# Sliding-window attention in a two-layer decoder kernel: value differences in place of two selects, weight splits on VectorE, and constants placed in earlier memory

## The chip, the cores and the metric

The kernel runs on one core of one Trainium2 chip, in one launch. The metric is the device time in microseconds; the median over several runs counts. Beside these runs one execution is profiled, and all rows below are from that execution.

## The reference

Two layers work on 512 rows of 1024 columns in fp32: an mLSTM layer, then a sliding-window attention layer with 16 query heads on 4 key/value heads, each layer with a post-norm, a squared-ReLU MLP (4096 wide) and a gated embedding. The change touches the attention layer. Cut to it:

```python
def swa_sink_attention(x, pos, k_sh, v_sh, w_q, b_q, sinks, w_o, b_o):
    q = partial_rope((x @ w_q + b_q).reshape(B, S, 16, 64), pos)
    kb, vb = banded(k_sh, nb), banded(v_sh, nb)      # block before, own block: 2 x 128 rows
    scores = einsum('bnqkgd,bnskd->bnkgqs', q, kb) * 64 ** -0.5
    diff = qi + 128 - si                             # qi: 0..127, si: 0..255
    valid = (diff >= 0) & (diff < 128) & (not before the first row)
    scores = where(valid, scores, -inf)
    m = maximum(max(scores), sink)
    e = exp(scores - m)
    probs = e / (sum(e) + exp(sink - m))
    out = einsum('bnkgqs,bnskd->bnqkgd', probs, vb).reshape(B, S, 1024)
    return out @ w_o + b_o
```

A query at place q of its block of 128 rows sees, of the block before, the places s > q, and of its own block, the places s <= q. So for each place s exactly one of the two blocks is seen.

## The kernel before

Rows come in four tiles of 128 (t = 0 to 3). Every product that needs fp32 is made of three matmuls (`mm3`, lines 88 to 90): the high and the low part of the weight against the high and the low part of the data, without low by low. So each weight matrix of 128 x 1024 is loaded into `wraw` (SyncE's DMA queue, line 83), and `split` makes `whi` from it on ScalarE (line 76) and `wlo` as the difference on another engine (line 77). `load_w` takes that engine as an argument: VectorE by default, GpSimd for `w_kv`, `w_q` and the first half of `w_o`. There are three `wraw` buffers and six each of `whi` and `wlo`.

The order of instructions on each engine is not the order of the code: a scheduler in the build sets it, engine by engine, and each engine then works through its own row in order. Memory is handed out by pools that open and close like a stack from the left or the right side; a tile in a pool opened later waits, tile by tile, for the last use of what lay in the same place.

The stage ahead of the attention layer is the first layer's gated embedding (`ple`, lines 709 to 737). Its tiles `pj` and `xr` lie in the pool `ps7`, along with the MLP's operands `S1`, `S23`, `S4A` and `T`, which are no longer used by then. When that pool closes, `pk` opens in its place, for what the attention layer keeps: the keys `KH` and `KL`, the values `vph` and `vpl` (high and low, one of each per tile), the biases `kvb` and `bq`. Value tiles have 64 zero columns ahead of and behind each head's 64, so that one matmul can write one head into the upper and another into the lower half of the output; these zeros are written by GpSimd (line 755).

The key/value projection then runs over four tiles (lines 792 to 811) into two accumulator banks. VectorE adds the bias out of the bank (`kv`, line 796) and rotates the keys (lines 779 to 782); TensorE transposes them (line 803), and ScalarE and VectorE write them as `KH` and `KL`.

Then, for each of the four key/value heads, `q_group` computes the queries (line 824 adds their bias, GpSimd rotates them, lines 833 and 834 write them into `QS`), and `attend` does the attention of a head's four query heads on one tile. In `attend` the scores of both blocks are computed, and VectorE copies the block before into the own block where the mask says so (line 850). So a row holds 128 scores, each of one block or the other. VectorE takes the maximum (line 851), and lines 856 to 859 make from it the maximum with the sink, its negative, and the exponent of the sink. ScalarE takes the exponentials (line 865), TensorE transposes the probabilities (line 873), and `ah` and `al` are their high and low parts. The two blocks' parts are taken apart again by four selects on GpSimd (lines 884 and 887), and each goes with its block's values (lines 893 to 895). The attend of one head and the query groups of the next are mixed by the scheduler.

Of the kernel before, what the change touches and what calls it, by code (L numbers as in the profile page):

```python
# [10 lines left out]
F32 = mybir.dt.float32  # L11
F32R = mybir.dt.float32r
# [3 lines left out]
ALU = mybir.AluOpType  # L16
# [14 lines left out]
KVH = 4  # L31
HD = 64
# [7 lines left out]
ASCALE = 0.125  # L40
# [5 lines left out]
def yoco_kernel(ctx: ExitStack, tc: tile.TileContext, A: dict, out: bass.AP):  # L46
    nc = tc.nc
    V, ACT, PE, GP = nc.vector, nc.scalar, nc.tensor, nc.gpsimd

    def pool(name, bufs=1, stack=ctx, **kw):  # L50
        return stack.enter_context(tc.tile_pool(name=name, bufs=bufs, **kw))

    base = pool("base")
# [14 lines left out]
    def tp_bank():  # L68
        return bank("tp")

    def f32(t):
        return t.bitcast(F32)


    def split(raw, n, hi, lo, eng=V):
        ACT.copy(hi, raw)  # L76
        eng.tensor_sub(lo, raw, f32(hi))  # L77

    def load_w(src, n, eng=V):
        raw = wpool.tile([P, 1024], F32, tag="raw", name="wraw", bufs=3)  # L80
        hi = wpool.tile([P, 1024], F32R, tag="whi", name="whi", bufs=6)
        lo = wpool.tile([P, 1024], F32R, tag="wlo", name="wlo", bufs=6)
        nc.sync.dma_start(raw[:, :n], src)
        split(raw[:, :n], n, hi[:, :n], lo[:, :n], eng)
        return hi, lo

    def mm3(o, lh, ll, rh, rl, start, stop):
        PE.matmul(o, lh, rh, start=start, stop=False)  # L88
        PE.matmul(o, lh, rl, start=False, stop=False)  # L89
        PE.matmul(o, ll, rh, start=False, stop=stop)  # L90
# [323 lines left out]
    sinkb = base.tile([P, KVH, 2, 2], F32, name="sinkb")  # L414
# [72 lines left out]
    sp = {}  # L487
# [44 lines left out]

    def seven_pools(i, side):
        sctx7 = ExitStack()
        ps = sp["s"] = pool(f"ps7{i}", stack=sctx7, side=side, reuse_waits="tile")
        sp["S1"] = [ps.tile([P, 4, 256], F32R, name=f"S1{x}") for x in "hl"]
        sp["S23"] = [ps.tile([P, 2, 4, 256], F32R, name=f"S23{x}") for x in "hl"]
        sp["S4A"] = [ps.tile([P, 2, 4, 256], F32R, name=f"S4A{x}") for x in "hl"]
        sp["T"] = ps.tile([P, 2, 512], F32, name="T")
        return sctx7  # L540
# [205 lines left out]
    pk = pool("pk", stack=kctx, side="right", reuse_waits="tile")  # L746
    KH = pk.tile([P, KVH, S], F32R, name="KH")
    KL = pk.tile([P, KVH, S], F32R, name="KL")
    VW = HD * (2 * KVH + 1)
    vph = [pk.tile([P, VW], F32R, name=f"vph{t}") for t in range(NT)]  # L750
    vpl = [pk.tile([P, VW], F32R, name=f"vpl{t}") for t in range(NT)]
    for t in range(NT):
        for vv in (vph[t], vpl[t]):
            for j in range(KVH + 1):
                GP.memset(f32(vv)[:, 2 * HD * j:2 * HD * j + HD], 0.0)
    kvb = pk.tile([P, 512], F32, name="kvb")
    nc.gpsimd.dma_start(kvb, A["kv_b"].partition_broadcast(P))
# [14 lines left out]
    pb = pool("pb", stack=bctx, side="right", reuse_waits="tile")  # L772
# [16 lines left out]
            mm3(ps, XH[:, k, tsl(t)], XL[:, k, tsl(t)], wh[:, sl], wl[:, sl], k == 0, k == KD - 1)  # L789
        return ps  # L790

    w = [load_w(A["w_kv"][0, c], 1024, GP) for c in range(4)]
    for t in range(NT):
        ps = proj512(t, w)
        kv = pb.tile([P, 512], F32, tag="bh", name="kv", bufs=2)
        V.tensor_add(kv, ps, kvb)  # L796
        kk = kv[:, 0:256].rearrange("p (h d) -> p h d", d=HD)
        rope(kk, t, KVH, V)
        kd = pb.tile([P, KVH, 2, HD], F32, tag="bl", name="kd", bufs=2)
        ACT.copy(kd, kk.unsqueeze(2).broadcast_to([P, KVH, 2, HD]))  # L800
        pt = tp_bank()
        for h in range(KVH):
            PE.transpose(pt[:, tsl(h)], kd[:, h].rearrange("p a d -> p (a d)"), ident)
        pv = pt.rearrange("p (h s) -> p h s", s=P)
        ACT.copy(KH[:, :, tsl(t)], pv)
        V.tensor_sub(KL[:, :, tsl(t)], pv, f32(KH)[:, :, tsl(t)])
        v = kv[:, 256:512].rearrange("p (h d) -> p h d", d=HD)
        vh = vph[t][:, HD:].rearrange("p (h d) -> p h d", d=2 * HD)[:, :, 0:HD]
        vl = vpl[t][:, HD:].rearrange("p (h d) -> p h d", d=2 * HD)[:, :, 0:HD]
        ACT.copy(vh, v)  # L810
        V.tensor_sub(vl, v, vh.bitcast(F32))
# [24 lines left out]
    def attend(gi, t):  # L836
        scs = []
        smax = pb.tile([P, 2, 2], F32, tag="smax", name="smax", bufs=2)
        for pr in range(2):
            k0 = max(t - 1, 0) * P  # L840
            ps = bank("sc")
# [9 lines left out]
            V.tensor_reduce(smax[:, :, pr], cur, AX.X, ALU.max)  # L851
            scs.append(cur)
        sk = sinkb[:, gi].rearrange("p pr par -> p par pr")
        m = pb.tile([P, 2, 2], F32, tag="am", name="am", bufs=2)
        nm = pb.tile([P, 2, 2], F32, tag="anm", name="anm", bufs=2)
        V.scalar_tensor_tensor(m, smax, ASCALE, sk, ALU.mult, ALU.max)
        V.tensor_scalar(nm, m, -1.0, None, ALU.mult)
        es = pb.tile([P, 2, 2], F32, tag="es", name="es", bufs=2)
        V.tensor_sub(es, sk, m)
# [14 lines left out]
        ah = pb.tile([P, 4, P], F32R, tag="ah", name="ah", bufs=2)  # L874
        al = pb.tile([P, 4, P], F32R, tag="al", name="al", bufs=2)
        pTv = pT.rearrange("p (h q) -> p h q", q=P)
        ACT.copy(ah, pTv)
        V.tensor_sub(al, pTv, f32(ah))
        parts = []
        if t > 0:  # L880
            bh = pb.tile([P, 4, P], F32R, tag="bh", name="bh", bufs=2)
            bl = pb.tile([P, 4, P], F32R, tag="bl", name="bl", bufs=2)
            for o, i_ in ((bh, ah), (bl, al)):
                GP.affine_select(out=o, in_=f32(i_), pattern=[[0, 4], [-1, P]], compare_op=ALU.is_ge, fill=0.0, base=-1, channel_multiplier=1)
            parts.append((t - 1, bh, bl))
            for o in (ah, al):
                GP.affine_select(out=o, in_=f32(o), pattern=[[0, 4], [1, P]], compare_op=ALU.is_ge, fill=0.0, base=0, channel_multiplier=-1)
        parts.append((t, ah, al))
        po = bank("pt")
        for i_, (kb, h_, l_) in enumerate(parts):  # L890
            for par in range(2):
                c0 = 2 * HD * gi + (HD if par == 0 else 0)
                mm3(po[:, :256], vph[kb][:, c0:c0 + P], vpl[kb][:, c0:c0 + P],
                    h_[:, 2 * par:2 * par + 2, :], l_[:, 2 * par:2 * par + 2, :],
                    i_ == 0 and par == 0, i_ == len(parts) - 1 and par == 1)
        pov = po[:, :256].rearrange("p (a q) -> p a q", a=2)
# [2 lines left out]
        V.tensor_sub(dl, pov, f32(dh))  # L899

    def load_q(gi):
        return [load_w(A["w_q"][gi, c], 1024, GP) for c in range(2)]

    w = load_q(0)
    for t in range(NT):
        q_group(0, t, w)
    for gi in range(KVH - 1):
        w = load_q(gi + 1)
# [121 lines left out]
```

## Time and profile before

| | us |
|---|---|
| three runs | 1225.95, 1220.97, 1225.16; median 1225.16 |
| profiled execution, its own time | 1223.72 |
| its span, first to last instruction | 1222.0 |
| TensorE busy | 1185.8 (97%) |
| VectorE busy | 877.2 (72%) |
| ScalarE busy | 586.6 (48%) |
| GpSimd busy | 148.1 (12%) |
| mean granted clock of TensorE | 0.991 of full speed |

In the rows, PE is TensorE, PEld its weight loads, DVE VectorE, ACT ScalarE, POOL GpSimd and SP SyncE. A row of the timeline gives the start and the duration in us, the engine, the line, the operation, what is written and read, a count where equal neighbours are merged, and in brackets the idle time ahead of it and what ended that. A row of the windows view gives for a stretch of time its length, then busy time and count of each engine, the granted clock, the DMA share and GB/s. Matmuls overlap, so the step from one start to the next says what one costs. The attention layer lies between about 600 and 800 us.

### The profile page before, as it was taken

The page shows a single profiled execution, that of the slowest core. Times are in us where ns is not written, and L with a number is a line of the kernel's source. Part 1 is how long each engine was busy: PE and PEld are TensorE (multiplying, and loading weights), DVE is VectorE, ACT ScalarE, POOL GpSimd, SP SyncE. Part 2 cuts the span into 40 slices and gives each one's busy share as a digit, 9 for nine tenths or more (in the row PEclk, how much of TensorE's full clock was granted, in tenths as well). Part 3 has the DMA queues.
Part 4 walks back from the last instruction along what each step waited for, and adds up shares of the span by engine and source line. Part 5 has one row for each costly group of instructions (what it writes and reads, how often), then busy time and mean ns, then how long its engine had stood idle before and what let it go on. Part 6 is the DMA issues. An engine that isn't in the chain of part 4 may idle for free.

```text
span 1222.0 us, 15691 instructions
## 1 busy us (share of the span) xinstructions
PE 1185.8 (97%) x5918; PEld 1007.5 (82%) x5918; DVE 877.2 (72%) x1445; ACT 586.6 (48%) x1014; POOL 148.1 (12%) x245
## 2 busy tenths in 40 slices
PE   8999999999999999999989989989999999999998
PEld 8799998888888888887878888779888888888876
DVE  6555566777487598699674788586956948969974
ACT  4645551565464463554333555335645446447431
POOL 1011021100000000001254564310000000000100
PEclk9999999999999999999999999999999999999999
DMA  7322224414406225026152111153250340531411
GB/s 245 98 86 67 85 79 172 173 35 148 128 1 206 70 68 178 31 68 191 55 178 70 53 53 36 45 217 118 65 178 34 121 155 1 174 102 35 150 58 52
DMA packets 35708, 124.55 MB, mean 102 GB/s; under 512 B 4064, under 2 KB 4592, under 8 KB 35632
## 3 DMA queue, kind: packets, MB, share of 16 engines
q1 hardware_dynamic: 33552, 116.46, 29.3%
q0 software_dynamic: 2080, 7.09, 1.9%
q8 instruction: 46, 0.75, 0.2%
q14 instruction: 30, 0.25, 0.1%
HBM read 119.34 MB, written 4.19 MB: 101 GB/s over the span
## 4 chain that ended last, share of the span: by engine, by line
PE 84%; DVE 7%; issue 3%; ACT 3%; DMA 2%; POOL 1%; SPq 0%; DVEq 0%; ACTq 0%; POOLq 0%
PE mm L88 26%; PE mm L90 26%; PE mm L89 26%; DVE wlo L77 1%; ACT pr L865 1%; DMA xraw<-in_xT_dram 1%; ACT whi L76 1%; PE tp L129 1%; DVE QS L834 1%; DVE smax L851 1%; PE tp L88 1%; DVE sc L850 1%; PE tp L89 1%; PE tp L90 1%; POOL wlo L77 1%
## 5 line engine op out<-in xcount | busy, mean ns | idle before, releaser
L76 ACT CAST whi<-wraw 128x1024 fp32r<-128x1024 f32 (+1 forms) x168 | 173.7, 1037 | 242.4 <-PE mm L90 136.2
L77 DVE TENSOR_TENSOR wlo<-wraw,whi 128x1024 fp32r<-128x1024 f32 (+1 forms) x152 | 184.5, 1216 | 125.8 <-ACT whi L76 124.8
L88 PE MATMUL mm<-XH,whi 128*128 128x512 f32 (+1 forms) x640 | 235.3, 370 | 1.5 <-ACT ot L230 1.2
L89 PE MATMUL mm<-XL,whi 128*128 128x512 f32 (+1 forms) x640 | 235.8, 369 | 0.0
L90 PE MATMUL mm<-XH,wlo 128*128 128x512 f32 (+1 forms) x640 | 235.8, 369 | 0.0
L88 PE MATMUL mm<-whi,XH 128*128 128x512 f32 (+2 forms) x424 | 148.1, 350 | 9.0 <-DVE kv L796 4.1
L89 PE MATMUL mm<-wlo,XH 128*128 128x512 f32 (+2 forms) x424 | 147.3, 348 | 0.0
L90 PE MATMUL mm<-whi,XL 128*128 128x512 f32 (+2 forms) x424 | 146.3, 348 | 0.0
L88 PEld LDWEIGHTS mm<-XH,whi 128*128 128x128 f32 x640 | 120.7, 190 | 22.0 <-ACT ot L230 1.7
L90 PEld LDWEIGHTS mm<-XH,wlo 128*128 128x128 f32 x640 | 121.2, 189 | 20.1
L89 PEld LDWEIGHTS mm<-XL,whi 128*128 128x128 f32 x640 | 121.2, 189 | 19.6
L76 ACT CAST whi<-rb 128x1024 fp32r<-128x1024 f32 x80 | 84.0, 1051 | 101.1 <-PE mm L89 54.6
L77 DVE TENSOR_TENSOR wlo<-rb,whi 128x1024 fp32r<-128x1024 f32 x80 | 97.5, 1223 | 39.0 <-ACT whi L76 39.0
L88 PEld LDWEIGHTS mm<-whi,XH 128*128 128x128 f32 x424 | 81.9, 193 | 18.1 <-issue 4.5
L89 PEld LDWEIGHTS mm<-wlo,XH 128*128 128x128 f32 x424 | 82.1, 194 | 7.9 <-issue 1.5
L90 PEld LDWEIGHTS mm<-whi,XL 128*128 128x128 f32 x424 | 82.0, 194 | 6.7 <-issue 0.8
L651 POOL DMA_DIRECT2D A11h<-in_mlp_ln_g_dram x2 | 1.2, 580 | 589.4 <-PE mm L90 589.4
L89 PE MATMUL mm<-wlo,S23h 128*128 128x512 f32 x128 | 50.7, 396 | 0.0
L89 PE MATMUL mm<-wlo,S4Ah 128*128 128x512 f32 x128 | 50.6, 395 | 0.0
L88 PE MATMUL mm<-whi,S23h 128*128 128x512 f32 x128 | 50.6, 395 | 0.0
L88 PE MATMUL mm<-whi,S4Ah 128*128 128x512 f32 x128 | 50.6, 395 | 0.0
L90 PE MATMUL mm<-whi,S4Al 128*128 128x512 f32 x128 | 50.3, 395 | 0.0
(302 smaller groups left out, 2356.6 us busy)
## 6 DMA issues: line engine op xcount, KB each, us to landing
wraw<-in_w_up_dram SPq DMA_DIRECT2D x64, 512.0 KB, 3.6
rb<-in_w_down_dram SPq DMA_DIRECT2D x48, 512.0 KB, 4.4
wraw<-in_w_down_dram SPq DMA_DIRECT2D x16, 512.0 KB, 3.7
wraw<-in_w_gate_dram SPq DMA_DIRECT2D x16, 512.0 KB, 3.6
wraw<-in_w_vo_dram SPq DMA_DIRECT2D x19, 412.0 KB, 3.3
wraw<-in_w_qk_dram SPq DMA_DIRECT2D x8, 512.0 KB, 4.3
wraw<-in_w_out_dram SPq DMA_DIRECT2D x8, 512.0 KB, 3.9
wraw<-in_w_q_dram SPq DMA_DIRECT2D x8, 512.0 KB, 3.6
```

The lines of the kernel that those rows point to most:

```text
L76: ACT.copy(hi, raw)
L77: eng.tensor_sub(lo, raw, f32(hi))
L88: PE.matmul(o, lh, rh, start=start, stop=False)
L89: PE.matmul(o, lh, rl, start=False, stop=False)
L90: PE.matmul(o, ll, rh, start=False, stop=stop)
L129: PE.transpose(pt[:, tsl(j)], src[:, tsl(b + j)], ident)
L651: nc.gpsimd.dma_start(v, A[n][i].partition_broadcast(P))
L834: V.tensor_sub(QS[other, hs, tsl(t)], pv[own], f32(QS)[own, hs, tsl(t)])
L850: V.copy_predicated(cur, mk, prev)
L851: V.tensor_reduce(smax[:, :, pr], cur, AX.X, ALU.max)
L865: ACT.activation(pt_[:, par, pr, :], scs[pr][:, par, :], AF.Exp, scale=ASCALE, bias=nm[:, par, pr:pr + 1], accum_out=sm[:, par, pr:pr + 1])
```

## The change

Instead of splitting the probabilities into the two blocks' parts, all of them go with the block before, and those of the own block go, a second time, with the difference between the own block's values and those of the block before: the sum of p v_before over all places, plus the sum of p (v_own - v_before) over the places s <= q. Two of four selects are left. `vown` holds the values of tiles 0 to 2, `vstep` the differences of tiles 1 to 3, each high and low. Moreover, all weight splits of the attention layer are on VectorE; the negative of the maximum comes from one operation, with a negated copy of the sinks (`nsink`); `seven_pools` opens two pools, `ps7` for the operands and `ring` for `rb`, `xr` and `pj`; and the biases stand ahead of the values in `pk`.

```diff
     def seven_pools(i, side):
         sctx7 = ExitStack()
-        ps = sp["s"] = pool(f"ps7{i}", stack=sctx7, side=side, reuse_waits="tile")
+        ps = pool(f"ps7{i}", stack=sctx7, side=side, reuse_waits="tile")
+        sp["s"] = pool(f"ring{i}", stack=sctx7, side=side, reuse_waits="tile")
...
     VW = HD * (2 * KVH + 1)
-    vph = [pk.tile([P, VW], F32R, name=f"vph{t}") for t in range(NT)]
-    vpl = [pk.tile([P, VW], F32R, name=f"vpl{t}") for t in range(NT)]
-    for t in range(NT):
-        for vv in (vph[t], vpl[t]):
-            for j in range(KVH + 1):
-                GP.memset(f32(vv)[:, 2 * HD * j:2 * HD * j + HD], 0.0)
     kvb = pk.tile([P, 512], F32, name="kvb")
     nc.gpsimd.dma_start(kvb, A["kv_b"].partition_broadcast(P))
     bq = pk.tile([P, D], F32, name="bq")
     nc.gpsimd.dma_start(bq, A["b_b_q"].partition_broadcast(P))
+    nsink = pk.tile([P, KVH, 2, 2], F32, name="nsink")
+    V.tensor_scalar(nsink, sinkb, -1.0, None, ALU.mult)
+
+    def vparts(name):
+        pair = [pk.tile([P, VW], F32R, name=f"{name}{x}") for x in "hl"]
+        for v in pair:
+            GP.memset(f32(v)[:, 0:2 * HD * KVH].rearrange("p (h d) -> p h d", d=2 * HD)[:, :, 0:HD], 0.0)
+            GP.memset(f32(v)[:, 2 * HD * KVH:], 0.0)
+        return pair
+
+    vown = [vparts(f"vo{t}") for t in range(NT - 1)]
+    vstep = [None] + [vparts(f"vs{t}") for t in range(1, NT)]
...
-    w = [load_w(A["w_kv"][0, c], 1024, GP) for c in range(4)]
+    w = [load_w(A["w_kv"][0, c], 1024) for c in range(4)]
+
+    def put_v(pair, v):
+        both_parts([x[:, HD:].rearrange("p (h d) -> p h d", d=2 * HD)[:, :, 0:HD] for x in pair], v)
...
-        ACT.copy(vh, v)
-        V.tensor_sub(vl, v, vh.bitcast(F32))
+        if t < NT - 1:
+            put_v(vown[t], v)
+        if t > 0:
+            dv = pb.tile([P, KVH, HD], F32, tag="dv", name="dv", bufs=2)
+            V.tensor_sub(dv, v, vlast)
+            put_v(vstep[t], dv)
+        vlast = v
...
-        V.scalar_tensor_tensor(m, smax, ASCALE, sk, ALU.mult, ALU.max)
-        V.tensor_scalar(nm, m, -1.0, None, ALU.mult)
+        nsk = nsink[:, gi].rearrange("p pr par -> p par pr")
+        V.scalar_tensor_tensor(nm, smax, -ASCALE, nsk, ALU.mult, ALU.min)
         es = pb.tile([P, 2, 2], F32, tag="es", name="es", bufs=2)
-        V.tensor_sub(es, sk, m)
+        V.tensor_add(es, sk, nm)
...
-        parts = []
-        if t > 0:
+        if t == 0:
+            parts = [(vown[0], ah, al)]
+        else:
             bh = pb.tile([P, 4, P], F32R, tag="bh", name="bh", bufs=2)
             bl = pb.tile([P, 4, P], F32R, tag="bl", name="bl", bufs=2)
             for o, i_ in ((bh, ah), (bl, al)):
-                GP.affine_select(out=o, in_=f32(i_), pattern=[[0, 4], [-1, P]], compare_op=ALU.is_ge, fill=0.0, base=-1, channel_multiplier=1)
-            parts.append((t - 1, bh, bl))
-            for o in (ah, al):
-                GP.affine_select(out=o, in_=f32(o), pattern=[[0, 4], [1, P]], compare_op=ALU.is_ge, fill=0.0, base=0, channel_multiplier=-1)
-        parts.append((t, ah, al))
+                GP.affine_select(out=o, in_=f32(i_), pattern=[[0, 4], [1, P]], compare_op=ALU.is_ge, fill=0.0, base=0, channel_multiplier=-1)
+            parts = [(vown[t - 1], ah, al), (vstep[t], bh, bl)]
...
-        return [load_w(A["w_q"][gi, c], 1024, GP) for c in range(2)]
+        return [load_w(A["w_q"][gi, c], 1024) for c in range(2)]
...
-    w = [load_w(A["w_o"][0, c], 1024, GP) for c in range(4)]
+    w = [load_w(A["w_o"][0, c], 1024) for c in range(4)]
```

The scheduler sets the order anew, so rows move. On GpSimd, from the end of the first MLP (`rs` is the norm's reciprocal root) to the load of the key/value bias, before:

```order
L138 TENSOR_TENSOR rs<-rs,nhalf 128x1 x4
L77 TENSOR_TENSOR wlo<-wraw,whi 128x1024 x6
L755 MEMSET vph_5262 128x64 x5
L755 MEMSET vpl_5266 128x64 x5
L755 MEMSET vph_5263 128x64 x5
L755 MEMSET vpl_5267 128x64 x5
L755 MEMSET vph_5264 128x64 x5
L755 MEMSET vpl_5268 128x64 x5
L755 MEMSET vph_5265 128x64 x5
L755 MEMSET vpl_5269 128x64 x5
L757 DMA kvb<-in_kv_b_dram 128x512
```

And now, at the same place:

```order
L121 DMA bc<-in_b_b_o_dram 128x1024
L138 TENSOR_TENSOR rs<-rs,nhalf 128x1 x4
L752 DMA kvb<-in_kv_b_dram 128x512
L754 DMA bq<-in_b_b_q_dram 128x1024
L761 MEMSET vo0h 128x4x64
L762 MEMSET vo0h 128x64
L761 MEMSET vo0l 128x4x64
```

The six splits and all memsets stood ahead of the bias; now the bias loads stand ahead of the memsets, and the splits are gone from this engine.

On VectorE, from the gated embedding's last tiles (`xr`, `res`) to the first bias addition of the key/value projection (`kv`), before:

```order
L726 TENSOR_TENSOR xr<-mm,bc 128x512
L736 SCALAR_TENSOR_TENSOR res_1747<-res_1747,bc 128x1024
L134 TENSOR_TENSOR XL<-tp,XH 128x4x128
L728 TENSOR_TENSOR xr<-xr,pj 128x512
L134 TENSOR_TENSOR XL<-tp,XH 128x4x128
L729 TENSOR_TENSOR res_1748<-res_1748,xr 128x512
L736 SCALAR_TENSOR_TENSOR res_1748<-res_1748,bc 128x1024
L134 TENSOR_TENSOR XL<-tp,XH 128x4x128
L796 TENSOR_TENSOR kv<-mm,kvb 128x512 x2
```

And now:

```order
L77 TENSOR_TENSOR wlo<-wraw,whi 128x1024
L730 TENSOR_TENSOR res_1747<-res_1747,xr 128x512
L77 TENSOR_TENSOR wlo<-wraw,whi 128x1024
L134 TENSOR_TENSOR XL<-tp,XH 128x4x128
L77 TENSOR_TENSOR wlo<-wraw,whi 128x1024
L727 TENSOR_TENSOR xr<-mm,bc 128x512
L737 SCALAR_TENSOR_TENSOR res_1747<-res_1747,bc 128x1024
L134 TENSOR_TENSOR XL<-tp,XH 128x4x128 x2
L77 TENSOR_TENSOR wlo<-wraw,whi 128x1024
L729 TENSOR_TENSOR xr<-xr,pj 128x512
L730 TENSOR_TENSOR res_1748<-res_1748,xr 128x512
L756 TENSOR_SCALAR nsink<-sinkb 128x16
```

The next row is the first `kv` addition, alone; the last tile's `res` and `XL` follow behind it. Four of the splits that came from GpSimd stand here, two stand earlier, four among the key/value additions, and six later.

Two of these six on VectorE, in the middle of the attention (`sc` are scores, `q` the query bias, `anm` the negated maximum):

```order
L77 TENSOR_TENSOR wlo<-wraw,whi 128x1024
L865 COPY_PREDICATED sc<-mask,sc 128x2x128
L866 TENSOR_REDUCE smax<-sc 128x2
L839 TENSOR_TENSOR q<-mm,bq 128x256
L77 TENSOR_TENSOR wlo<-wraw,whi 128x1024
L871 SCALAR_TENSOR_TENSOR anm<-smax,nsink 128x4
```

Before, no split stood among these rows of VectorE, and an operation `am` and another `anm` made the negated maximum.

More of the change, by code (lines that the diff above doesn't have):

```diff
@@ L790, in proj512 @@
         return ps
-    w = [load_w(A["w_kv"][0, c], 1024, GP) for c in range(4)]
+    w = [load_w(A["w_kv"][0, c], 1024) for c in range(4)]
+    def put_v(pair, v):
+        both_parts([x[:, HD:].rearrange("p (h d) -> p h d", d=2 * HD)[:, :, 0:HD] for x in pair], v)
+    vlast = None
     for t in range(NT):
@@ L807, in yoco_kernel @@
         v = kv[:, 256:512].rearrange("p (h d) -> p h d", d=HD)
-        vh = vph[t][:, HD:].rearrange("p (h d) -> p h d", d=2 * HD)[:, :, 0:HD]
-        vl = vpl[t][:, HD:].rearrange("p (h d) -> p h d", d=2 * HD)[:, :, 0:HD]
-        ACT.copy(vh, v)
-        V.tensor_sub(vl, v, vh.bitcast(F32))
+        if t < NT - 1:
[5 more added lines that the diff above has]
+        vlast = v
     qbank = [None]
@@ L853, in attend @@
         sk = sinkb[:, gi].rearrange("p pr par -> p par pr")
-        m = pb.tile([P, 2, 2], F32, tag="am", name="am", bufs=2)
         nm = pb.tile([P, 2, 2], F32, tag="anm", name="anm", bufs=2)
-        V.scalar_tensor_tensor(m, smax, ASCALE, sk, ALU.mult, ALU.max)
-        V.tensor_scalar(nm, m, -1.0, None, ALU.mult)
+        nsk = nsink[:, gi].rearrange("p pr par -> p par pr")
+        V.scalar_tensor_tensor(nm, smax, -ASCALE, nsk, ALU.mult, ALU.min)
         es = pb.tile([P, 2, 2], F32, tag="es", name="es", bufs=2)
-        V.tensor_sub(es, sk, m)
+        V.tensor_add(es, sk, nm)
         ACT.activation(es, es, AF.Exp)
@@ L883, in attend @@
             for o, i_ in ((bh, ah), (bl, al)):
-                GP.affine_select(out=o, in_=f32(i_), pattern=[[0, 4], [-1, P]], compare_op=ALU.is_ge, fill=0.0, base=-1, channel_multiplier=1)
-            parts.append((t - 1, bh, bl))
-            for o in (ah, al):
-                GP.affine_select(out=o, in_=f32(o), pattern=[[0, 4], [1, P]], compare_op=ALU.is_ge, fill=0.0, base=0, channel_multiplier=-1)
-        parts.append((t, ah, al))
+                GP.affine_select(out=o, in_=f32(i_), pattern=[[0, 4], [1, P]], compare_op=ALU.is_ge, fill=0.0, base=0, channel_multiplier=-1)
+            parts = [(vown[t - 1], ah, al), (vstep[t], bh, bl)]
         po = bank("pt")
-        for i_, (kb, h_, l_) in enumerate(parts):
+        for i_, (vv, h_, l_) in enumerate(parts):
             for par in range(2):
                 c0 = 2 * HD * gi + (HD if par == 0 else 0)
-                mm3(po[:, :256], vph[kb][:, c0:c0 + P], vpl[kb][:, c0:c0 + P],
+                mm3(po[:, :256], vv[0][:, c0:c0 + P], vv[1][:, c0:c0 + P],
                     h_[:, 2 * par:2 * par + 2, :], l_[:, 2 * par:2 * par + 2, :],
```

## The prediction

> **What bounds the kernel now.** I read the head of the page first, then the chain, then busy time by stage, then who TensorE waits for.
>
> ```profile
> span 1222.0 us, 15691 instructions
> PE 1185.8 (97%) x5918; PEld 1007.5 (82%) x5918; DVE 877.2 (72%) x1445; ACT 586.6 (48%) x1014; POOL 148.1 (12%) x245
> PE 84%; DVE 7%; issue 3%; ACT 3%; DMA 2%; POOL 1%; SPq 0%; DVEq 0%; ACTq 0%; POOLq 0%
> ```
>
> TensorE sets the time: it is busy for 97% of the span, and 84% of the chain is its own work. The change adds and removes no matmul: a tile with t > 0 has two groups of six value matmuls before and after. So it can only move time where TensorE stands still or runs at a lower clock. Three stages of the windows view, around the attention layer, with busy time of PE, PEld, DVE, ACT, POOL, then the granted clock:
>
> ```profile
> 605.00:635.00 30.00, 29.97 (x147) 24.74 (x146) 23.77 (x25) 11.47 (x16) 16.33 (x30) 1.00 0.47 158
> 640.00:660.00 20.00, 18.34 (x87) 15.65 (x88) 9.08 (x22) 7.43 (x12) 6.60 (x3) 0.83 0.19 61
> 720.00:740.00 20.00, 17.38 (x130) 16.89 (x129) 17.66 (x43) 9.05 (x31) 14.70 (x25) 0.91 0.16 54
> ```
>
> Ahead of the key/value projection TensorE has no idle time (29.97 of 30). In the attention layer it idles, and the clock falls. The waits of TensorE alone, 595 to 800 us (total, times, longest):
>
> ```profile
> PE sc L845 <- ACT pr L865: 4.7, 5, 2.1
> PE mm L88 <- DVE kv L796: 4.1, 1, 4.1
> PE mm L88 <- DVE q L824: 3.2, 3, 2.0
> PE tp L828 <- DVE QS L834: 1.9, 2, 1.4
> PE tp L803 <- DVE KL L806: 0.8, 1, 0.8
> PE pt L89 <- POOL bl L884: 0.4, 1, 0.4
> ```
>
> That is 15.1 us in 13 waits; the terms below are taken from these rows.
>
> **Part 1: the constants of the layer come early.** POOL, then DVE and PE, in the timeline:
>
> ```profile
> 580.02 2.70 POOL L138 TENSOR_TENSOR rs<-rs,nhalf 128x1 f32<-128x1 f32 x2 [12.41 <-DVE rs L137]
> 621.68 11.37 POOL L77 TENSOR_TENSOR wlo<-wraw,whi 128x1024 fp32r<-128x1024 f32 x4 [12.49 <-ACT whi L76]
> 632.98 0.49 POOL L755 MEMSET vph<- 128x64 f32 x5
> 636.45 0.60 POOL L757 DMA_DIRECT2D kvb<-in_kv_b_dram  x1
> 640.82 1.29 DVE L796 TENSOR_TENSOR kv<-mm,kvb 128x512 f32<-128x512 f32 x2 [4.59 <-DMA kvb<-in_kv_b_dram]
> 641.66 0.77 PE L88 MATMUL mm<-whi,XH 128*128 128x512 f32 x1 [4.07 <-DVE kv L796]
> ```
>
> The reader is to see a queue: four weight splits hold POOL until 633, forty memsets follow, and only then is the load of the key/value bias issued, at 636.45. Two projection tiles fill the only two accumulator banks, DVE cannot empty the first without the bias, and TensorE stands for 4.07 us. In the new order the two bias loads stand straight behind the four rs operations, the last of which ends at 582.7, and ahead of all memsets. What they wait for is the built program's answer: matmuls of the last quarter of the first MLP that read S23, which the next row shows done at 556.5.
>
> ```profile
> 556.15 0.40 PE L90 MATMUL mm<-whi,S23l 128*128 128x512 f32 x1
> 642.00:644.00 2.00, 2.00 (x6) 1.52 (x6) 1.72 (x11) 1.18 (x3) 0.00 (x0) 0.50 0.00 0
> 646.00:648.00 2.00, 2.00 (x7) 1.57 (x6) 0.00 (x0) 0.00 (x0) 0.00 (x0) 0.61 0.00 0
> ```
>
> From issue to DVE's start is 4.4 us (636.45 to 640.82), so the bias is there near 588, 50 us early; the memsets hide in the same 50 us. The idle time also cost clock: about 0.50 from 641.66 to 647, 5.8 us of matmuls at half speed, so 2.9 us more. Part 1 is worth 4.07 + 2.9 = 7.0 us. What is late next is DVE's addition of the first tile, which now stands behind one more split; that is a rival below.
>
> **Part 2: sixteen weight splits leave POOL for DVE.** The groups, 600 to 800 us (count, busy, mean ns of one, idle before):
>
> ```profile
> L77 POOL TENSOR_TENSOR wlo<-wraw,whi 128x1024 fp32r<-128x1024 f32 x16 | 40.5, 2547 | 51.1 <-ACT whi L76 51.1
> L77 DVE TENSOR_TENSOR wlo<-wraw,whi 128x1024 fp32r<-128x1024 f32 x7 | 8.5, 1220 | 6.2 <-ACT whi L76 6.2
> L887 POOL TENSOR_SCALAR_AFFINE_SELECT al<-al 128x512 fp32r<-128x512 f32 x12 | 8.6, 715 | 0.0
> L811 DVE TENSOR_TENSOR vpl<-kv,vph 128x256 fp32r<-128x256 f32 x4 | 1.7, 419 | 0.0
> ```
>
> A split takes 2.55 us on POOL and 1.22 on DVE. But DVE does not go free while POOL works. One place, word for word:
>
> ```profile
> 722.12 2.35 POOL L77 TENSOR_TENSOR wlo<-wraw,whi 128x1024 fp32r<-128x1024 f32 x1
> 722.20 2.29 DVE L857 TENSOR_SCALAR anm<-am 128x4 f32<-128x4 f32 x1
> 724.41 0.15 DVE L859 TENSOR_TENSOR es<-sinkb,am 128x4 f32<-128x4 f32 x1
> 724.48 0.41 DVE L824 TENSOR_TENSOR q<-mm,bq 128x256 f32<-128x256 f32 x1
> 724.95 0.39 PE L88 MATMUL mm<-whi,XH 128*128 128x256 f32 x1 [1.99 <-DVE q L824]
> 726.00:730.00 4.00, 4.00 (x23) 4.00 (x22) 3.83 (x7) 1.27 (x6) 4.00 (x7) 0.57 0.61 206
> ```
>
> An operation on 4 columns lasts 2.29 us, as long as POOL's split, where its neighbour of the same size takes 0.15; the query addition behind it is late, TensorE waits 1.99 us, and the clock then stands at 0.57 for 4 us (4 x 0.43 = 1.7 lost). Without the split on POOL both go: 3.7 us. Two smaller places of the same kind:
>
> ```profile
> 658.16 2.44 DVE L780 TENSOR_TENSOR tb<-kv,sin 128x64 f32<-128x64 f32 x1
> 661.58 0.66 PE L803 MATMUL tp<-ident,kd 128*128 128x128 f32 x4 [0.81 <-DVE KL L806]
> 677.50 0.83 DVE L856 SCALAR_TENSOR_TENSOR am<-smax,sinkb 128x4 f32<-128x4 f32 x1
> 680.93 0.39 PE L845 MATMUL sc<-KH,QS 128*128 128x256 f32 x1 [2.06 <-ACT pr L865]
> ```
>
> The first gives 0.8 us. In the second 0.7 (0.83 less 0.15) of the 2.06 is the block, and the rest is the exponential's path.
>
> The cost: sixteen times 1.22 is 19.5 us of DVE. Six splits stand ahead of the first kv addition, where TensorE has 29.97 of 30 us of work to cover them, and where four POOL splits held DVE up before; these I cost at nothing. Ten stand behind it: four in the key/value projection, six among the attention operations; 10 x 1.22 = 12.2 us. Bounds: 0 if all fall into DVE's idle time (640 to 660 it is busy for 9.08 of 20), 12.2 if each is on the path. The nearest rows are POOL's blocks after 641: 1.2, 2.2, 0.7 and 2.1 us (such a row less its unblocked size), 6.2 in all, for which TensorE waited 0.8 + 0.7 + 2.0 = 3.5, more than half. Those fell where they happened to fall; the new ones have places in DVE's order, two of them ahead of a query addition or a maximum. I take a third, 4.1.
>
> **Part 3: two selects go, value differences come.** The first value group now reads ah and al unselected, so it waits for DVE alone; the 0.4 us of the wait on bl goes. Twenty-four selects (715 ns and less each) leave POOL. Added on DVE are three differences and two more low parts of 256 columns, 5 x 0.42 = 2.1 us (the L811 row), and two copies on ACT. They stand in the key/value projection, where a tile gives TensorE 24 matmuls at some 0.23 us, 5.5 us of cover; without that cover they would cost 2.1. nsink is one operation of 16 columns: nothing. An attend has one operation less on DVE, 0.15 us (the L859 row), ahead of the exponentials. Five waits end on these: 0.7. Bounds are 0 and the whole 4.7.
>
> **The ring pool** also lets six loads of w_down go ahead of w_up loads, once per layer. The four w_up matrices needed first stand ahead of them, so nothing; at most it delays the norm's constants after attention.
>
> **Sum.** 7.0 + 3.7 + 0.8 + 0.7 + 0.4 + 0.7 = 13.3; less 4.1 is 9.2. The profiled execution took 1223.72 us (span 1222.0 and 1.72 around it): 1223.72 - 9.2 = 1214.5. It lies 1.44 under the median of the three runs (1225.16), which themselves spread over 5 us, so I leave it at 1214.5. Half a per cent, 6.1 us, is about what can be told from no change here; faster means under 1219.0.
>
> The clock terms (2.9 and 1.7) come from rows. The Trainium skill, "TensorE: Matmul & The Clock Gate", section "HAM oscillation", puts the rule as no idle gaps of TensorE above about 3.4 us. By it the gap of 1.99 us should have kept the full clock, and the sum would give 1216.2, inside the forecast's own range; the trace differs (0.57 behind that gap), and I go by the trace.
>
> **Rivals.**
>
> *New waits eat most of it.* DVE is full where it matters: 17.66 of 20 us from 720 to 740. If the kv addition is late by 2 us at the place of the old gap, and two more idle times of about 2 us appear with 1.7 us of clock each, then 13.3 - 2 - 7.4 = 3.9 is left: 1219.8. For it: a split now stands four operations ahead of that addition, and its cast waits for a buffer. Against: it needs over 5 us of delay before TensorE, which has a second tile to compute, notices at all. 0.22.
>
> *Slower.* DVE becomes the bound: every one of the ten late splits holds an addition or maximum for which TensorE waits, 12.2 us, and five of these waits pass 2 us and cost 1.7 each, 8.5; 20.7 - 13.3 = 7.4, so 1231. For it: the wait for casts, 51.1 us, was harmless on POOL and would not be on DVE, which works in order. It decides from 1.3 us per split upward. 0.06.
>
> *More than forecast.* The path from scores to exponentials relaxes too: the other 1.4 of the 2.06, 1.9 on QS, 1.2 of the rest on q, and the clock after two such gaps, 3.4, go: 7.9 more, and half the split cost, 2: 1204.6. Against: 720 to 740 stays crowded on DVE. 0.14.
>
> *It doesn't do what it says*: the bias is still late since its buffer is released late. The order and the wait on S23 speak against. Then 7.0 is missing: 1221.5. 0.03.
>
> **Numbers.** Forecast 1214.5 with 0.55, its own range 1210 to 1219. The range over all, 1205 to 1221, takes in the larger part of the rivals on both sides. Faster: 0.52 of the forecast, 0.14, and 0.08 of the first rival, 0.74. Within 0.5%: 0.03 + 0.14 + 0.03 = 0.20. Slower 0.06.
>
> **What would show it.** After: kvb's load on POOL near 583 and no TensorE wait on kv above 1 us; clock 1.00 from 635 to 660; no DVE operation of 4 to 64 columns above 1 us; no wlo on POOL; twelve pairs of selects; DVE's busy time within 5 us of 877. I am wrong if waits on q or QS add up to more than the 5.1 us of now, or if a wait on a split's cast stands in DVE's rows with 2 us or more ahead of a kv or q addition.

## The result and the profile after

The changed kernel takes 1205.74 us (median of four runs, 1204.11 to 1206.17), the kernel before 1224.27 beside it (four runs, 1220.97 to 1225.95). The ratio is 0.9849, with a 95% interval of 0.9826 to 0.9873: 18.5 us less, twice the 9.2 of the sum. The profiled execution took 1205.69 us (span 1204.0).

The head of the page, then three stages of the windows view of the changed kernel (the columns as before):

```profile
span 1204.0 us, 15649 instructions
PE 1178.7 (98%) x5918; PEld 1001.0 (83%) x5918; DVE 879.0 (73%) x1451; ACT 587.5 (49%) x1016; POOL 95.8 (8%) x189
```

```profile
640.00:660.00 20.00, 19.57 (x133) 17.86 (x132) 12.87 (x27) 8.87 (x14) 2.22 (x8) 1.00 0.33 106
660.00:680.00 20.00, 18.93 (x152) 17.99 (x151) 13.71 (x35) 9.74 (x29) 5.33 (x17) 1.00 0.17 54
720.00:740.00 20.00, 19.92 (x144) 18.45 (x145) 16.78 (x49) 12.38 (x48) 6.31 (x17) 1.00 0.09 27
```

The granted clock is 1.00 in each; before it was 0.83 from 640 to 660 and 0.91 from 720 to 740, where TensorE was busy for 18.34 and 17.38 us. The changed kernel runs ahead of the other here, so the same stretch of time does not hold quite the same work: its last scores start at 756.5 us, and before at 769.8. The waits of TensorE in the changed kernel, 595 to 800 us (total, times, longest; the first six):

```profile
PE mm L88 <- DVE q L839: 2.2, 4, 0.7
PE pt L89 <- DVE al L892: 1.3, 2, 0.9
PE mm L88 <- DVE res L157: 0.6, 1, 0.6
PE pt L88 <- DVE QS L911: 0.5, 1, 0.5
PE tp L843 <- DVE KL L818: 0.4, 1, 0.4
PE pt L88 <- ACT ah L891: 0.4, 1, 0.4
```

No wait is longer than 0.9 us. The 4.07 us on `kv` are gone, as are the single waits of 2.06 on the exponentials and 1.99 on `q`. GpSimd's load of the bias and VectorE's third addition of it in the timeline, then VectorE's groups of the splits and of the negated maximum, 600 to 800 us:

```profile
582.25 0.59 POOL L752 DMA_DIRECT2D kvb<-in_kv_b_dram  x1
...
642.87 0.69 DVE L808 TENSOR_TENSOR kv<-mm,kvb 128x512 f32<-128x512 f32 x1 [1.21 <-PE mm L90]
```

```profile
L77 DVE TENSOR_TENSOR wlo<-wraw,whi 128x1024 fp32r<-128x1024 f32 x26 | 31.6, 1228 | 6.4 <-ACT whi L76 6.4
...
L871 DVE SCALAR_TENSOR_TENSOR anm<-smax,nsink 128x4 f32<-128x4 f32 x16 | 2.8, 172 | 0.3
```

The bias is loaded at 582, and VectorE now waits for TensorE at that place, not TensorE for VectorE. A maximum takes 172 ns where before the two operations took 318 and 381 on average:

```profile
L857 DVE TENSOR_SCALAR anm<-am 128x4 f32<-128x4 f32 x16 | 6.1, 381 | 0.4
L856 DVE SCALAR_TENSOR_TENSOR am<-smax,sinkb 128x4 f32<-128x4 f32 x16 | 5.1, 318 | 0.3
```

So the waits that the prediction named went, and others went too. The experiments ask which part did it, and whether the work or the order did.

### The profile page after: what moved, and what is told of

Same layout as the page of the kernel before. It is cut to its first block, busy times and chain, and to the rows that moved or that the text cites. A ratio compares the mean times of both kernels' runs of the same rounds, so it can differ in the third digit from the quotient of the medians.

```text
span 1204.0 us, 15649 instructions
## 1 busy us (share of the span) xinstructions
PE 1178.7 (98%) x5918; PEld 1001.0 (83%) x5918; DVE 879.0 (73%) x1451; ACT 587.5 (49%) x1016; POOL 95.8 (8%) x189
## 5 line engine op out<-in xcount | busy, mean ns | idle before, releaser
L77 DVE TENSOR_TENSOR wlo<-wraw,whi 128x1024 fp32r<-128x1024 f32 (+1 forms) x168 | 204.1, 1218 | 125.2 <-ACT whi L76 124.2
L633 DVE TENSOR_TENSOR res<-res,mm 128x512 f32<-128x512 f32 x72 | 48.6, 682 | 1.5 <-PE mm L90 1.0
```

The costliest lines, as they stand in the source:

```text
L633: V.tensor_add(r[:, h], r[:, h], bank)
```

## The experiments

Three theories. Theory 1: the work makes the time, the late bias and GpSimd's splits above all. Theory 2: the surplus belongs to a part (value differences, maximum), and the parts add up. Theory 3: the scheduler makes another order of the attention layer out of any edit, and the order makes a good part of the time. Ratios are to the kernel before, run beside each kernel on the same chip; differences in us are the ratio's distance times that kernel's median there (1221.92, 1222.55 and 1222.76 in the three groups below).

### Each part alone on the kernel before

*Early constants.*

```diff
-        ps = sp["s"] = pool(f"ps7{i}", ...)
+        ps = pool(f"ps7{i}", ...)
+        sp["s"] = pool(f"ring{i}", ...)
...
+    kvb = pk.tile(...); nc.gpsimd.dma_start(kvb, ...)
+    bq = pk.tile(...); nc.gpsimd.dma_start(bq, ...)
     vph = [pk.tile(...) for t in range(NT)]
...
-    kvb = pk.tile(...); nc.gpsimd.dma_start(kvb, ...)
-    bq = pk.tile(...); nc.gpsimd.dma_start(bq, ...)
```

> The kernel before with one edit: the second pool and the biases ahead of the values. Theory 1 (the gain is GpSimd's splits leaving VectorE alone; the bias wait is a term of its own of 7.0 us): the TensorE wait of 4.07 us on kv goes, the clock is 1.00 from 640 to 660, the blocks of 2.3 us on small VectorE operations stay; 7 us less than before, 1215 to 1219. Theory 2 (the terms add up as in the prediction, and the surplus of some 9 us comes from the value part): the same 7 us. Theory 3 (any edit reorders the attention stage, and the order makes the time): the wait goes but others come; anywhere between 3 us more and 10 less.

*Splits on VectorE.*

```diff
-    w = [load_w(A["w_kv"][0, c], 1024, GP) for c in range(4)]
+    w = [load_w(A["w_kv"][0, c], 1024) for c in range(4)]
...
-        return [load_w(A["w_q"][gi, c], 1024, GP) for c in range(2)]
+        return [load_w(A["w_q"][gi, c], 1024) for c in range(2)]
...
-    w = [load_w(A["w_o"][0, c], 1024, GP) for c in range(4)]
+    w = [load_w(A["w_o"][0, c], 1024) for c in range(4)]
```

> The kernel before with one edit: the sixteen weight splits on VectorE. Theory 1: the blocks go, and the bias load too comes earlier, since the memsets ahead of it wait only for VectorE's last additions near 625 and no longer for four splits until 633; the wait on kv falls from 4.07 to under 2 us, no wait behind it reaches 2 us, the clock stays full: 11 to 16 us less, 1208 to 1213. Theory 2 (the terms of the prediction: 3.7 + 0.8 + 0.7 gained, 4.1 paid, the bias still late): 1 us less, 1222 to 1224. Theory 3: between the two, with new waits of 2 us at other places.

*Value differences*, with their memsets (the lines of the change from `vparts` to `parts`, nothing else):

```diff
-            parts.append((t - 1, bh, bl))
-            for o in (ah, al):
-                GP.affine_select(out=o, in_=f32(o), ...)
-        parts.append((t, ah, al))
+            parts = [(vown[t - 1], ah, al), (vstep[t], bh, bl)]
```

> The kernel before with one edit: value differences in place of two selects (with the memsets that go with them). Theory 1: the blocks of GpSimd's splits and the late bias stay, so within 2 us of before, 1222 to 1226. Theory 2 (the surplus comes from here and from the maximum): 5 to 9 us less, 1215 to 1219, the waits on the exponentials under 2.5 us in sum. Theory 3: anywhere within 5 us of before.

*Negated maximum.*

```diff
-        V.scalar_tensor_tensor(m, smax, ASCALE, sk, ALU.mult, ALU.max)
-        V.tensor_scalar(nm, m, -1.0, None, ALU.mult)
+        V.scalar_tensor_tensor(nm, smax, -ASCALE, nsk, ALU.mult, ALU.min)
```

> The kernel before with one edit: the negated maximum in one operation. Theory 1: within 1.5 us of before. Theory 2: the waits on the exponentials fall from 4.7 us to about 2, 2 to 4 us less, 1220 to 1222. Theory 3: within 5 us of before, either way, with another order of the attention stage.

| alone on before | ratio | interval | us |
|---|---|---|---|
| early constants | 0.9968 | 0.9957 to 0.9980 | 3.9 less |
| splits on VectorE | 0.9956 | 0.9941 to 0.9972 | 5.4 less |
| value differences | 1.0033 | 1.0018 to 1.0048 | 4.0 more |
| negated maximum | 0.9976 | 0.9963 to 0.9989 | 2.9 less |

Together 8.2 us less; all four at once give 18.5. So the parts do not add up, and theory 2 falls: its 2 to 4 less for the negated maximum came, but the value differences, for which it had 5 to 9 less, made the kernel slower. Theory 1 missed as well: 3.9 where 7 was expected of the early bias, 5.4 where 11 to 16 was expected of the splits. The waits with the early constants alone, then with the splits alone (longest ones of each):

```profile
PE sc L846 <- ACT pr L866: 5.0, 4, 2.6
PE tp L829 <- DVE QS L835: 4.0, 3, 1.8
PE mm L88 <- DVE res L157: 2.2, 1, 2.2
```

```profile
PE mm L88 <- DVE q L824: 5.8, 7, 2.2
...
PE pt L88 <- POOL bh L884: 1.4, 1, 1.4
...
PE mm L88 <- DVE kv L796: 0.9, 1, 0.9
```

With the constants early, the wait on `kv` is gone, but QS went from 1.9 to 4.0. With the splits on VectorE, the wait on `kv` fell to 0.9 although nothing was done for the bias (no split stands ahead of its load any more), and the waits on `q` grew from 3.2 to 5.8. The other two leave the bias late: with the value differences alone the wait on `kv` is 4.9 us, with the negated maximum alone it is 4.8, and the waits on QS grew to 4.2. So where an edit takes a wait away, others come at new places.

### Each part taken back from the changed kernel

The same edits the other way round (the diff of each is that of the change, reversed for the part named).

```diff
-        ps = pool(f"ps7{i}", ...)
-        sp["s"] = pool(f"ring{i}", ...)
+        ps = sp["s"] = pool(f"ps7{i}", ...)
...
-    kvb = pk.tile(...); nc.gpsimd.dma_start(kvb, ...)
-    bq = pk.tile(...); nc.gpsimd.dma_start(bq, ...)
...
     vstep = [None] + [vparts(f"vs{t}") for t in range(1, NT)]
+    kvb = pk.tile(...); nc.gpsimd.dma_start(kvb, ...)
+    bq = pk.tile(...); nc.gpsimd.dma_start(bq, ...)
```

> The changed kernel with one part taken back: one pool again, the biases behind the values. In the built order twenty-four memsets stand ahead of the bias load, and the first waits for VectorE's last addition to the residual (630.90 in the changed kernel); so the load is issued near 637 and lands near 641. Theory 1 (the wait on kv is a term of its own): a wait of 4 to 5 us on kv and half the clock behind it are back, 6 to 8 us more than the changed kernel, 1211 to 1214 (ratio to before 0.990 to 0.992). Theory 2 (a sum of the parts as measured alone): 4 us more, 0.988. Theory 3 (the changed kernel's order happens to be a good one, and any edit loses it): waits also appear after 660, 8 to 12 us more, above 0.992.

```diff
-    w = [load_w(A["w_kv"][0, c], 1024) for c in range(4)]
+    w = [load_w(A["w_kv"][0, c], 1024, GP) for c in range(4)]
```

(and so for `w_q` and `w_o`)

> The changed kernel with one part taken back: the sixteen weight splits on GpSimd again. Theory 1 (VectorE held up by GpSimd's splits is the main cost, and VectorE's own splits cost nothing): small VectorE operations of 2.3 us are back, TensorE waits of 2 us and a clock of 0.91 in two or three stretches of 20 us; 8 to 12 us more, ratio 0.992 to 0.995. Theory 2 (sum of the parts alone): 5.4 us more, 0.989. Theory 3: 8 to 12 us more, the waits at other places than the blocks.

```diff
-            parts = [(vown[t - 1], ah, al), (vstep[t], bh, bl)]
+            parts.append((t - 1, bh, bl))
+            for o in (ah, al):
+                GP.affine_select(out=o, in_=f32(o), ...)
+        parts.append((t, ah, al))
```

> The changed kernel with one part taken back: four selects per tile again, no value differences. Theory 1: the waits on bh and bl (2.1 us where the splits alone were moved) are back, and GpSimd's longer work slows VectorE a little; 2 to 5 us more, ratio 0.986 to 0.989. Theory 2 (sum of the parts alone; there it made the kernel 4 us slower): 4 us less, 0.982. Theory 3: 5 to 8 us more, with waits on q and QS too.

```diff
-        V.scalar_tensor_tensor(nm, smax, -ASCALE, nsk, ALU.mult, ALU.min)
+        V.scalar_tensor_tensor(m, smax, ASCALE, sk, ALU.mult, ALU.max)
+        V.tensor_scalar(nm, m, -1.0, None, ALU.mult)
```

> The changed kernel with one part taken back: the maximum and its negative in two operations. Theory 1: sixteen times 0.15 us on VectorE, 0 to 2 us more, ratio 0.985 to 0.987. Theory 2 (as alone): 3 us more, 0.987 to 0.988. Theory 3: 4 to 8 us more, waits of 1 to 2 us at places that have nothing to do with the maximum.

| changed kernel without | ratio | interval | us above the changed kernel (0.9849) |
|---|---|---|---|
| early constants | 0.9932 | 0.9907 to 0.9958 | 10.1 |
| splits on VectorE | 0.9895 | 0.9865 to 0.9924 | 5.6 |
| value differences | 0.9862 | 0.9837 to 0.9886 | 1.6 |
| negated maximum | 0.9925 | 0.9897 to 0.9953 | 9.3 |

The changed kernel was not run again beside these; its 0.9849 has an interval of 2.9 us to either side. So the 5.6 us of the splits are not quite clear of it (0.9865 against 0.9873), and the value differences make no difference that shows here. Without the early constants the bias is loaded late again (GpSimd in the timeline, then TensorE's waits) and the wait on `kv` is back, and one of 1.6 us on the exponentials as well:

```profile
633.47 0.59 POOL L763 DMA_DIRECT2D kvb<-in_kv_b_dram  x1
```

```profile
PE mm L88 <- DVE kv L807: 3.7, 1, 3.7
...
PE sc L859 <- ACT pr L878: 1.9, 2, 1.6
```

Without the splits on VectorE the blocks are back (the profiled execution of this kernel took 1216.73 us, 5.0 above its median):

```profile
L871 DVE SCALAR_TENSOR_TENSOR anm<-smax,nsink 128x4 f32<-128x4 f32 x16 | 5.9, 368 | 0.3
```

368 ns in place of 172. The odd one is the last: sixteen operations of 0.15 us, 2.4 us of VectorE, cost 9.3. Its waits and one window, without the negated maximum:

```profile
PE sc L858 <- ACT pr L878: 2.8, 4, 1.4
PE pt L89 <- DVE al L891: 2.7, 4, 0.8
PE pt L88 <- ACT ah L890: 2.0, 3, 0.7
...
PE pt L886 <- DVE am L869: 1.6, 1, 1.6
```

```profile
740.00:760.00 20.00, 14.89 (x96) 12.12 (x94) 14.28 (x45) 9.74 (x43) 4.25 (x6) 1.00 0.00 1
```

From 740 to 760 TensorE idles for 5.1 us (2.4 in the changed kernel, which is busy for 17.64 there, though not with quite the same work: its last scores start at 756.5, here at 765.3). The longest wait is the 1.6 us of transposes that read the scaled probabilities; the operation `am` that its row names stands just behind the scaling in VectorE's order. 0.15 us more per tile does not explain such waits by its size. That is what theory 3 says, but an order and a longer path changed together here. The next four kernels separate them.

### The work changed, the order held

In these kernels each engine's row of instructions is fixed: every instruction is queued behind its neighbour in the row of another kernel, so the scheduler has no choice. Only what the edit itself adds, removes or moves differs.

```diff
         yoco_kernel(tc, aps, out)
+        pin_order(tc)
...
+def pin_order(tc):
...
+        for a, b in zip(row, row[1:]):
+            tc.add_manual_dep(b, a.name, ...)
```

The first has the work of the early constants, in the order of before:

> The kernel before with the second pool and the early bias loads, each engine's row of instructions held as it was before; only the two bias loads move ahead on GpSimd. So the price of the late bias by itself. The prediction's term (4.07 us of wait, 2.9 of clock): 7.0 less, ratio 0.994. If the rest of the stage takes it back (the next addition or the next split late): 2 to 4 less, 0.997 to 0.998, with a new wait behind 645. If more hangs on it: 9 or more less, 0.992.

The second has all of the change but the value differences, in the order of before:

> The kernel before with the early biases, the splits on VectorE and the negated maximum in one operation, all rows held in the order of before (a split stands on VectorE where it stood on GpSimd). The work is that of the run without value differences (ratio 0.986); only the order differs. Theory 1 (the work makes the time): 14 to 18 us less, 0.985 to 0.988. Theory 3 (the order that the scheduler finds for the new work makes a good part): 6 to 10 us less, 0.992 to 0.995, with waits of 1 to 2 us on q, QS or the exponentials at the old places.

The third has the maximum in two operations, in the order of the changed kernel:

> The changed kernel with the maximum and its negative in two operations, all rows held in the changed kernel's order. Left to the scheduler the same work gave a ratio of 0.9925, some 9 us above the changed kernel. Theory 1 (the longer path to the exponentials costs it): again 0.991 to 0.993. Theory 3 (the operation of 0.15 us costs little, and the 9 us came from the other order that it brought about): 0 to 2.4 us more than the changed kernel, 0.985 to 0.987.

The fourth makes late splits twice, in the order of the changed kernel:

```diff
-        split(raw[:, :n], n, hi[:, :n], lo[:, :n], eng)
+        split(raw[:, :n], n, hi[:, :n], lo[:, :n], eng); again and V.tensor_sub(lo[:, :n], raw[:, :n], f32(hi[:, :n]))
...
-        return [load_w(A["w_q"][gi, c], 1024) for c in range(2)]
+        return [load_w(A["w_q"][gi, c], 1024, again=True) for c in range(2)]
...
-    w = [load_w(A["w_o"][0, c], 1024) for c in range(4)]
+    w = [load_w(A["w_o"][0, c], 1024, again=True) for c in range(4)]
```

> The changed kernel with twelve of its splits on VectorE (w_q and w_o) made twice, one straight behind the other, all rows in the changed kernel's order: 12 x 1.22 = 14.6 us more on VectorE. It measures what a split on VectorE costs there. If VectorE's idle time covers them: 0 to 2 us more, ratio 0.985 to 0.987. If a third of them shows, as the prediction took it: 5 us more, 0.989. If nearly all: 12 to 15 us more, 0.995 to 0.997.

| | ratio | interval | us |
|---|---|---|---|
| early constants, order of before | 0.9938 | 0.9919 to 0.9957 | 7.6 less than before |
| all but value differences, order of before | 0.9919 | 0.9905 to 0.9934 | 9.9 less than before |
| the same work, the scheduler's order | 0.9862 | 0.9837 to 0.9886 | 16.9 less than before |
| two operations, order of the changed kernel | 0.9877 | 0.9864 to 0.9889 | 3.4 above the changed kernel |
| the same work, the scheduler's order | 0.9925 | 0.9897 to 0.9953 | 9.3 above the changed kernel |
| twelve splits twice, order of the changed kernel | 0.9936 | 0.9924 to 0.9948 | 10.6 above the changed kernel |

Two pairs have the same work and differ in order alone: 7.0 us in the one (0.9919 and 0.9862), 5.9 in the other (0.9877 and 0.9925). In neither do the intervals touch. Theory 3 is shown, and beside it theory 1 for a part: with the order held, the work brings 9.9 us. The 3.4 us of the two operations lie above the 0 to 2.4 that theory 3 had for them, by ratios whose intervals overlap a little.

Held in the order of before, the early bias takes away its own wait and no other of note, so holding the order adds no wait that shows; these are the four largest sums (before: 4.7, 3.2, 1.9, 0.8 on the same four), then the window at the old gap:

```profile
PE sc L846 <- ACT pr L866: 4.8, 5, 2.1
PE mm L88 <- DVE q L825: 3.2, 3, 2.0
PE tp L829 <- DVE QS L835: 1.9, 2, 1.5
PE tp L804 <- DVE KL L807: 0.8, 1, 0.8
```

```profile
635.00:660.00 25.00, 24.18 (x161) 21.91 (x159) 12.13 (x29) 9.68 (x15) 11.58 (x12) 1.00 0.28 85
```

What the order does, at one place. First the waits of the second kernel (order of before), then of the same work in the scheduler's order:

```profile
PE sc L850 <- ACT pr L869: 3.7, 5, 1.7
PE mm L88 <- DVE q L829: 3.6, 5, 1.2
PE tp L833 <- DVE QS L839: 2.6, 4, 1.7
PE pt L877 <- DVE pr L873: 1.6, 2, 1.3
```

```profile
PE mm L88 <- DVE q L829: 2.9, 5, 0.7
PE tp L833 <- DVE QS L839: 1.1, 2, 0.6
...
PE sc L850 <- ACT pr L869: 0.2, 1, 0.2
```

3.7 us on the exponentials became 0.2. All rows of the two lists add up to 14.2 and 6.8 us; the spans, 1211.2 and 1203.8, differ by 7.4. TensorE in the timeline at the first of these waits, order of before:

```profile
662.83 0.28 PE L850 MATMUL sc<-KH,QS 128*128 128x256 f32 x1
...
664.40 0.39 PE L88 MATMUL mm<-whi,XH 128*128 128x256 f32 x1 [0.25 <-DVE q L829]
...
668.46 0.28 PE L851 MATMUL sc<-KL,QS 128*128 128x256 f32 x1
670.47 0.38 PE L850 MATMUL sc<-KH,QS 128*128 128x256 f32 x1 [1.73 <-ACT pr L869]
```

And in the scheduler's order:

```profile
663.88 0.28 PE L850 MATMUL sc<-KH,QS 128*128 128x256 f32 x1
...
665.70 0.39 PE L88 MATMUL mm<-whi,XH 128*128 128x256 f32 x1
...
669.63 0.39 PE L88 MATMUL mm<-whi,XH 128*128 128x256 f32 x1 [0.34 <-DVE q L829]
...
672.37 0.28 PE L850 MATMUL sc<-KH,QS 128*128 128x256 f32 x1
```

Between the first scores and the scores that need a bank back from the exponentials there stands one query group of matmuls in the first kernel (from 664.40), and one and most of another in the second (from 665.70 and from 669.63). In the first, TensorE wants the bank 5.9 us after the first scores (670.47 less the wait of 1.73, less 662.83) and stands still; in the second it wants it after 8.5 us and finds it free. The same matmuls stand in both, in other places. The exponentials themselves come no sooner: the first starts 6.7 us after the first scores in the one kernel and 6.5 in the other (669.51 and 670.37 in ScalarE's rows).

The doubled splits give the price of a split on VectorE: 10.6 us for 12 x 1.22 = 14.6 us of work, seven tenths (with the intervals of both ratios, half to nearly all). Their longest waits and the window behind the first bias addition:

```profile
PE mm L88 <- DVE q L839: 5.0, 7, 1.9
PE mm L88 <- DVE kv L808: 2.2, 1, 2.2
```

```profile
635.00:660.00 25.00, 22.21 (x142) 19.62 (x142) 19.58 (x40) 10.11 (x17) 1.95 (x7) 1.00 0.33 106
```

VectorE is busy for 19.58 of 25 us there, and a `kv` addition is late by 2.2. These are splits on top of those that the change put there, on an engine that is already full, each ahead of a matmul that reads it; that the first ten cost as much is not shown.

## Why the prediction was right and wrong, point by point

**The sum.** 12.9 of its 13.3 gained, less 4.1, belong to what the second kernel of the last group contains: 8.8 (the other 0.4 is the wait on `bl`). It measured 9.9 (8.1 to 11.6 by its interval). For the order of before the sum was right. What failed is the step from the terms to the time: every term was a wait of the old order, made shorter, and the sum had no term for a new order, though the order is the scheduler's and the change gave it other work. That term measured 7.0 us, and for want of it the time lies outside the forecast's own range of 1210 to 1219. The remaining 1.6 go with the value differences, and the intervals do not tell them from nothing.

**Part 1, 7.0.** Held in order it measured 7.6 (5.3 to 9.9). The bias load stands at 582.25 (forecast: near 583), the clock is 1.00 in the windows behind it, and the 2.9 us of clock are part of what came. Nothing was late next: the wait on `kv` is not among those left.

**Part 2, 5.2 less 4.1.** With the order held, splits and maximum together brought 9.9 - 7.6 = 2.3 us; the sum had 1.1 + 0.7 = 1.8. That fits, but the intervals of the two runs overlap, so a net of nothing would fit as well. Its two sides are less sure: the blocks went (172 ns where 318 and 381 had stood), and a late split, by the doubled ones, costs seven tenths of its time and not the third that was taken; if the ten cost as much, the blocks had cost more than the rows named. The trace supports that without proving it. Sixteen splits, 19.5 us, came to VectorE, and its busy time went from 877.2 to 879.0, so about that much of what had counted as busy was time blocked. By the means of its groups from 600 to 800 us, some 7 us of this lay ahead of the projection (the additions to `xr` and `res`), where TensorE did not wait, and some 11 behind, where the prediction's rows had 6.2. Not all of it was the splits' doing: with the splits alone moved, the two operations of the maximum still took 206 and 210 ns. The Trainium skill, "SBUF — State Buffer", section "Who interferes with whom", has GpSimd and VectorE share a pair of ports under an exclusive lock, which whoever issues first holds for the whole instruction; the 368 ns that return with the splits on GpSimd agree.

**Part 3, 0.4 and 0.7.** The wait on `bl` of 0.4 us went. One operation less per attend measured 3.4 us with the order held, by ratios whose intervals overlap a little; the two profiled spans differ by 1.7 (1205.7 and 1204.0). So 0.7 looks too small without being ruled out; 3.4 lies under the bound of 4.7. The path to the exponentials has one more piece that the prediction did not name: a table load of 1.28 us on ScalarE, which in the kernel before stands ahead of the exponentials that the wait of 2.06 ends on:

```profile
678.69 1.28 ACT L865 ACT_TABLE_LOAD   x1 [2.06 <-DVE es L859]
```

It stands there in the changed kernel too (670.04). What it would bring to make that load earlier was not tried.

**The rivals.** The time came out beside *more than forecast* (1204.6), and 0.7 us inside the range over all; that is luck, for the reason was another. The waits of that rival did go (2.06 on the exponentials, 1.9 on QS, and the clock behind them). But not by the way it told: with the shorter work in the old order 3.7 us on the exponentials and 2.6 on QS stayed; the order removed them. *New waits eat most of it* is what the early bias alone showed (3.9 of 7), but not the whole change. *Slower* and *doesn't do what it says* did not come, though the price of the doubled splits, 0.9 us each where *slower* begins at 1.3, shows that the first was nearer than 0.06 made it look.

**What would show it.** All signs of being right came: the bias load near 583, no wait on `kv`, clock 1.00, no small VectorE operation above 1 us, no `wlo` on GpSimd, twelve pairs of selects, VectorE's busy time within 5 us. They are signs of the terms; none of them asked whether the order was still the old one. Of the two signs of being wrong one came as well: at 664.49 a split on VectorE waits 3.59 us for its cast, and a `q` addition stands two rows behind it. It did no harm, since TensorE waits for no more than 0.43 us at a time from 655 to 672; the sign was badly chosen. The other did not: the waits on `q` and QS fell from 5.1 to 3.1 us.

**The clock.** By the rule of 3.4 us the sum would have been 1216.2. The runs go on disagreeing with it as a bound on the gap's length. By what the traces show in its place (last section), a gap of 2 us costs 1.7 us or nothing by where it falls, so the 1.7 behind the gap on `q` need not have come in every run (the mean granted clock of the kernel before was between 0.989 and 0.995 in its runs).

**Left open.** Which feature of the new work made the scheduler choose the better order, and whether value differences bring anything in a held order, was not tried; neither was the ring pool's effect on the loads by itself. No kernel was held in its own order; that holding an order costs nothing rests on the first held kernel, whose four largest waits are those of before to 0.1 us.

## What to carry to other kernels

Where a scheduler sets the order, price an edit first with the old order held, and then allow for the order as a term of its own: here it was worth 6 to 7 us, as much as the largest term of the sum, and the same four edits alone summed to 8.2 us where together they gave 18.5. An experiment that undoes one edit measures the edit and a new order together; fixing each engine's row to that of the other kernel separates them. When a wait goes, look for what fills the place: at the place shown, a result that came no sooner cost nothing once one more group of independent matmuls stood ahead of its reader.

## What the runs showed of the hardware

A gap of TensorE of about 2 us does not always cost clock. In the kernel with doubled splits a wait of 2.17 us up to 651.6 left the clock at 1.00, and one of 1.94 up to 720.8 was followed by a stretch at half speed (windows of 4 us at both places, the second pair at 0.78 and 0.79):

```profile
648.00:652.00 4.00, 1.83 (x16) 1.60 (x15) 3.97 (x5) 1.53 (x2) 0.00 (x0) 1.00 0.45 135
652.00:656.00 4.00, 3.80 (x31) 3.60 (x31) 3.97 (x10) 1.03 (x2) 0.95 (x3) 1.00 0.67 168
...
720.00:724.00 4.00, 3.21 (x20) 3.21 (x21) 3.93 (x7) 0.00 (x0) 1.84 (x5) 0.78 0.40 133
724.00:728.00 4.00, 3.96 (x28) 3.76 (x26) 3.36 (x9) 1.59 (x7) 1.20 (x2) 0.79 0.40 131
```

The loss is much the same each time it comes: 4 x 0.22 + 4 x 0.21 = 1.7 us here, 1.7 at 726 before, 1.8 in the windows of 20 us at 0.91. A gap's length does not say whether it comes.

The traces show what does. Each records when the granted clock changed, and within a trace these moments lie on a grid of 3.413 us: in the kernel before the clock falls to a half at 227.72, 640.73, 681.69, 726.06 and 763.61 us, which is 121, 12, 13 and 11 times 3.413 from one to the next, and it stays there for 3.41 us, behind the gap of 4.07 for twice that. Cut on this grid, what counts is how long TensorE was busy in one stretch:

| kernel, stretch | wait in it | TensorE busy | clock in the next stretch |
|---|---|---|---|
| doubled splits, 647.16 to 650.58 | part of 2.17 us | 2.29 of 3.42 us | 1.00 |
| doubled splits, 650.58 to 653.99 | the rest of it | 2.38 of 3.41 | 1.00 |
| doubled splits, 718.85 to 722.26 | 1.94 | 1.47 of 3.41 | 0.50 |
| before, 722.65 to 726.06 | 1.99 | 1.42 of 3.41 | 0.50 |

In the fourteen traces, from 30 to 1195 us, 31 stretches at full clock have TensorE busy for less than 48%, and half the clock follows each; of 26 between 48% and 60% it follows 6; of 4676 above that, none. So a gap of 2 us costs 1.7 us where it falls into one stretch, and nothing where the grid cuts it in two. From trace to trace the grid stands at another place: 2.4 us past a multiple of 3.413 in the kernel before, 0.8 in the changed one.

The Trainium skill, "TensorE: Matmul & The Clock Gate", section "What's actually happening", describes a window of 3413 ns that runs freely and does not start anew with the kernel; the grid agrees.
